# Start-up order, norm by one constant matmul, and the place of 24 modulation blocks in a two-layer diffusion backbone

## The chip, the cores and the metric

One core of a Trainium2 chip runs the whole kernel: TensorE (PE), VectorE (DVE), ScalarE (ACT), GpSimd (POOL) and the DMA queue that SyncE (SP) feeds. The metric is the device time of one execution in microseconds.

## The reference, cut to what matters

Two layers over 256 latent tokens and 256 context tokens of width 2048, all in float32. Layer 0 is a gated linear recurrence beside a short convolution, layer 1 a Hyena long convolution; a squared-ReLU mlp follows each. Every sublayer's input is normalised, scaled and shifted by a modulation vector that comes from the conditioning vector c.

```python
def rmsnorm(x, g):
    xf = x * lax.rsqrt(jnp.mean(x * x, axis=-1, keepdims=True) + EPS)
    return xf * g
for l in range(2):
    sh1, sc1, g1, sh2, sc2, g2 = split(silu(c) @ ada_w[l] + ada_b[l], 6)
    h = rmsnorm(x, norm_g[l, 0]) * (1.0 + sc1) + sh1
    if l == 0:   # the context goes through the same weights with its own modulation
        hc = rmsnorm(ctx, norm_g[0, 0]) * (1.0 + csc1) + csh1
        y = hgrn_conv_mixer(h, hc, ab_w_in, ..., ab_w_out)
    else:
        y = hyena_mixer(h, hy_in_w, ..., hy_out_w)
    x = x + g1 * y
    x = x + g2 * sq_relu_mlp(rmsnorm(x, norm_g[l, 1]) * (1.0 + sc2) + sh2, mlp_w1[l], mlp_w2[l])
return rmsnorm(x, final_g)
```

## The kernel before, in words

**Data.** Activations lie transposed: 16 k-tiles of 128 channels by 256 tokens. Every large product is three TensorE products of halves (high and low part of each operand): a weight tile of 1 MB is loaded into one of three buffers `raw`, ScalarE copies its high part (`whi`, L150) and VectorE makes the low part (`wlo`, L151). TensorE then runs high by high, high by low and low by high.

**Stages** of the profiled execution: phase 0, the first 3072 columns of ab_w_in for tokens and context (0 to 455 us); the other columns of that projection and the recurrence (to 785); its output projection (to 890); mlp(0) (to 1655); the hyena's input projection with its chain of transforms (to 2142); its output projection, called "ho" (to 2260); mlp(1) (to 3006); the last norm and the store.

**Phase 0** goes by k: `KBLOCKS` cuts the 16 k-tiles into stretches of 1, 3, 4 and 8, and each stretch adds its part to sums in SBUF (L611, L615). A stretch is a row of weight loads (L676); `block_mm` (L594, L597) multiplies each by the normalised tokens (side 0) and context (side 1). The input of k-tile kt, `h`, needs the norm of the tokens and two modulation vectors: `ada_start(kt)` loads two blocks of 1 MB and multiplies them on TensorE (L211, then L551 and L553); `h_make` turns x and the modulation into h (L562, L568, L570, L571). All k-tiles of the next stretch go through `ada_start` between the weight loads of a stretch, and `h_make` makes all of them at its end.

**Modulation blocks.** 192 blocks of 1 MB make the modulation, in the order of their index l\*96 + ch\*16 + kt. The first 32 are those of ada_start. The rest stand in a queue `ada_q` that `pump` and `pump_rate` empty at points set by hand: `RATES` says how many blocks a point takes off ("hy" in the hyena chain, "ho" in its output projection, ("m1", l) in the mlps). A block whose index is in `ON_PE` is multiplied by `ada_mm` on TensorE (L211, sums of rows L193, L194), any other by one VectorE instruction with a sum (L181). Loads (L162) go through `raw`, or in the mlps and the first output projection through two buffers of their own, `araw`. `pump_until` empties the queue up to the index that the next step needs.

**A norm** is `rstd_sum` (L324: squares times a constant column, giving 128x2), `rsqrt` (L304 to L312, integer start and three Newton steps on 128x2), and `rstd_fin` (L333: two diagonals; L337: a matmul that spreads them over all partitions). There are six: two in phase 0, and before mlp(0), the hyena, mlp(1) and the store. In phase 0 the squares of four k-tile quads are added by `qadd` (L527), one of three by GpSimd.

**The filter network** of the hyena (`filter_net`, L1053 to L1185) runs on GpSimd from the start of the kernel; `filter_tail` (L1124 on) uses it in mlp(0).

The order on each engine is the scheduler's, close to the order of the program text; loads are issued by SP in that order, and a load waits until its buffer is free.

## Time and profile before

| | us |
|---|---|
| median of three runs | 3024.0 (3020.43 to 3026.61) |
| the profiled execution, its own time | 3025.2 |
| its span in the trace | 3023.4 |
| TensorE busy | 2787.5 (92%) |
| VectorE busy | 2203.2 (73%) |
| ScalarE busy | 1241.5 (41%) |
| GpSimd busy | 1535.0 (51%) |
| mean DMA rate | 214 GB/s |

The shares are means over all stages. TensorE is nearly full over the mlps, so the stages in which it is not have to be read one by one, by windows. A row of the timeline gives the start, the duration and the engine of one or several equal instructions and, in brackets, how long the engine was idle before and what released it; an SPq row is the issue of a load and its wait for a buffer.

### The profile page before, as it was taken

The numbers are of one execution on the slowest core, as the hardware profiler recorded it, in microseconds if no ns is written. First come the engines' busy times: TensorE is split into PE (matmuls) and PEld (weight loads), VectorE is DVE, ScalarE is ACT, GpSimd is POOL, SyncE is SP. The second block draws the span as 40 slices with busy tenths as digits, with TensorE's granted clock in tenths as the row PEclk, the third lists the DMA queues.
The fourth block names the chain that finished last, engine by engine and source line by source line (L and its number), as shares of the span: only waits on it lengthen the run. The fifth ranks groups of instructions, "written<-read, shape, count | busy, mean of one in ns | idle before, by whom it ended". The sixth has DMA issues, their size and how long they took to land.

```text
span 3023.4 us, 44604 instructions
## 1 busy us (share of the span) xinstructions
PE 2787.5 (92%) x17728; PEld 2455.0 (81%) x17728; DVE 2203.2 (73%) x2632; ACT 1241.5 (41%) x1635; POOL 1535.0 (51%) x1718
## 2 busy tenths in 40 slices
PE   4887899999989999998999898889779999999997
PEld 3787899988988888887888788889777888888885
DVE  3565669998798878876778899999766555555555
ACT  3212224333445444353445454444335444344443
POOL 6999999999999999925000444554000000000000
PEclk8898899999999999999999899999999999999998
DMA  4766455445767887886876333333575555656553
GB/s 158 277 245 233 169 193 183 163 142 221 259 237 270 321 303 294 323 294 257 310 289 248 125 136 122 130 140 112 186 276 180 211 211 212 217 209 218 199 181 112
DMA packets 97569, 647.43 MB, mean 214 GB/s; under 512 B 11640, under 2 KB 15800, under 8 KB 21456
## 3 DMA queue, kind: packets, MB, share of 16 engines
q1 hardware_dynamic: 96176, 641.40, 58.2%
q0 software_dynamic: 1184, 3.18, 0.7%
q8 instruction: 139, 2.28, 0.3%
q14 instruction: 70, 0.57, 0.1%
HBM read 642.44 MB, written 2.10 MB: 213 GB/s over the span
## 4 chain that ended last, share of the span: by engine, by line
PE 64%; DVE 22%; DMA 5%; issue 3%; ACT 2%; POOL 2%; DVEq 0%; ACTq 0%; SPq 0%; POOLq 0%
PE acc L281 45%; PE acc L260 8%; DVE wlo L151 6%; PE aux L594 2%; PE acc L594 2%; DMA raw<-in_w 1%; DMA raw<-in_ho 1%; PE aux L295 1%; DVE raw L181 1%; PE aux L597 1%; DVE p L939 1%; DMA raw<-in_ada 1%; PE acc L597 1%; DVE p L937 1%; ACT whi L150 1%
## 5 line engine op out<-in xcount | busy, mean ns | idle before, releaser
L151 DVE TENSOR_TENSOR wlo<-raw,whi 128x1024 fp32r<-128x1024 f32 (+1 forms) x772 | 1011.8, 1315 | 514.2 <-ACT whi L150 509.5
L150 ACT ACTIVATE whi<-raw 128x1024 fp32r<-128x1024 f32 (+1 forms) x800 | 842.1, 1056 | 1163.3 <-PE acc L281 706.9
L1034 POOL TENSOR_TENSOR xT<-xT,rstd 128x256 f32<-128x256 f32 x6 | 5.3, 910 | 878.6 <-ACT rstd L449 878.6
L260 PE MATMUL acc<-hh,whi 128*128 128x258 f32 (+1 forms) x1408 | 406.4, 289 | 1.5 <-ACT whi L150 1.5
L260 PE MATMUL acc<-hh,wlo 128*128 128x258 f32 (+1 forms) x1408 | 400.5, 285 | 5.7 <-DVE wlo L151 5.3
L281 PE MATMUL acc<-whi,hh 128*128 128x512 f32 x1024 | 403.2, 399 | 2.2 <-ACT hh L442 2.2
L281 PE MATMUL acc<-whi,uh 128*128 128x512 f32 x1024 | 405.1, 396 | 0.0
L281 PE MATMUL acc<-whi,ul 128*128 128x512 f32 x1024 | 404.9, 395 | 0.0
L281 PE MATMUL acc<-whi,hl 128*128 128x512 f32 x1024 | 402.8, 398 | 0.2 <-DVE hl L443 0.2
L260 PE MATMUL acc<-hl,whi 128*128 128x258 f32 (+1 forms) x1408 | 398.7, 284 | 0.0
L281 PE MATMUL acc<-wlo,uh 128*128 128x512 f32 x1024 | 282.6, 396 | 8.9 <-DVE wlo L151 8.9
L281 PE MATMUL acc<-wlo,hh 128*128 128x512 f32 x1024 | 279.0, 394 | 0.0
L260 PEld LDWEIGHTS acc<-hh,wlo 128*128 128x128 f32 x1408 | 267.8, 190 | 8.5 <-DVE wlo L151 7.6
L260 PEld LDWEIGHTS acc<-hh,whi 128*128 128x128 f32 x1408 | 268.4, 191 | 6.5 <-issue 4.3
L260 PEld LDWEIGHTS acc<-hl,whi 128*128 128x128 f32 x1408 | 269.1, 191 | 0.9 <-issue 0.7
L181 DVE SCALAR_TENSOR_TENSOR araw<-araw,sil 128x2048 f32<-128x2048 f32 x102 | 249.4, 2446 | 0.0
L281 PEld LDWEIGHTS acc<-wlo,uh 128*128 128x128 f32 x1024 | 192.8, 188 | 54.7 <-DVE wlo L151 9.4
L281 PEld LDWEIGHTS acc<-whi,hh 128*128 128x128 f32 x1024 | 193.2, 189 | 47.8 <-ACT hh L442 3.7
L281 PEld LDWEIGHTS acc<-whi,hl 128*128 128x128 f32 x1024 | 193.8, 189 | 44.3 <-DVE hl L443 0.8
L281 PEld LDWEIGHTS acc<-wlo,hh 128*128 128x128 f32 x1024 | 193.0, 188 | 45.1
L281 PEld LDWEIGHTS acc<-whi,uh 128*128 128x128 f32 x1024 | 192.9, 188 | 45.0 <-issue 0.3
L281 PEld LDWEIGHTS acc<-whi,ul 128*128 128x128 f32 x1024 | 192.9, 188 | 44.5
(361 smaller groups left out, 5792.6 us busy)
## 6 DMA issues: line engine op xcount, KB each, us to landing
raw<-in_m SPq DMA_DIRECT2D x256, 1024.0 KB, 4.9
araw<-in_ada SPq DMA_DIRECT2D x102, 1024.0 KB, 5.8
raw<-in_ada SPq DMA_DIRECT2D x89, 1024.0 KB, 5.1
raw<-in_w SPq DMA_DIRECT2D x75, 1024.0 KB, 5.0
raw<-in_hy SPq DMA_DIRECT2D x48, 1024.0 KB, 4.9
raw<-in_ho SPq DMA_DIRECT2D x16, 1024.0 KB, 4.8
raw<-in_w SPq DMA_DIRECT2D x6, 768.0 KB, 6.4
raw<-in_c SPq DMA_DIRECT2D x4, 1024.0 KB, 4.7
```

Of the source, the lines that this page charges most:

```text
L150: nc.scalar.activation(out=hi[:, :w], in_=src, func=AF.Copy)
L151: e.tensor_tensor(out=lo[:, :w], in0=src, in1=hi[:, :w].bitcast(F32), op=ALU.subtract)
L181: self.hold(nc.vector.scalar_tensor_tensor(out=r, in0=r, scalar=0.5, in1=self.sil, op0=ALU.mult, op1=ALU.mult, accum_out=self.mod[:, idx:i ...
L260: m = nc.tensor.matmul(acc[:, :n], lhsT=w[:, s], rhs=x(kt, n), start=hn == 0 and j == 0 and pn == 0, stop=hn == 1 and j == 7 and pn == 2).ins
L281: nc.tensor.matmul(acc[th], lhsT=x(kt)[:, th * P:(th + 1) * P], rhs=w[:, j * 512:(j + 1) * 512], start=kt == 0 and w is hi and x is xhi, s ...
L295: nc.tensor.transpose(out=tp[:, j * T + th * P:j * T + th * P + P], in_=src[th][:, f * P:(f + 1) * P], identity=self.ident)
L594: nc.tensor.matmul(o, lhsT=w[:, e + half * P:e + half * P + P], rhs=x(kt), start=st, stop=sp)
L597: nc.tensor.matmul(o, lhsT=x(kt)[:, half * P:half * P + P], rhs=w[:, e:e + T], start=st, stop=sp)
L937: nc.vector.scalar_tensor_tensor(out=c3[:, :, 1:], in0=u3[:, :, :63], scalar=w0, in1=c3[:, :, 1:], op0=ALU.mult, op1=ALU.add)
L939: nc.vector.scalar_tensor_tensor(out=c3[:, :, :63], in0=u3[:, :, 1:], scalar=w2, in1=c3[:, :, :63], op0=ALU.mult, op1=ALU.add)
L1034: e.tensor_tensor(out=self.x[:, nt, :], in0=self.x[:, nt, :], in1=rstd, op=ALU.mult)
```

## The change

1. `KBLOCKS` becomes (1, 2, 5, 8): the second stretch has three weight loads of 1 MB, the third twelve of 0.625 MB; the fourth is as before.
2. At the beginning the first modulation blocks and weights are loaded into their own tiles (`fa`, `fw0`), and those of k-tiles 1 and 2 are issued ahead, in front of the filter network's loads. Squares and norm of the tokens come ahead of `ada_start(0)`; VectorE does all three sums; `ada_start(1)` stands ahead of the context's norm. In the stretches, `h` of a k-tile is made one weight load after its `ada_start`, for the last four on side 1 at the end of the third stretch.
3. `norm_rstd` multiplies the squares by a constant 128x128 matrix, which gives the sum on all partitions, and takes `rsqrt` at 128x256; diagonals, second matmul and copy are gone. All six norms use it.
4. Blocks 160 to 183 (of layer 1) are added to `ON_PE`. `RATES` takes 0.5 instead of 0.1 in the hyena chain and 0 instead of 1 in ho. `ada_stop` bounds what a stage may take, and `pump_to` empties up to it: 56 after phase 0, 72 before the first output projection, 160 in mlp(0), 184 in the hyena. The vector for VectorE's blocks (`make_sil`) is not made in the hyena.
5. `filter_net` is tied to the last h operation of k-tile 2 in the scheduler's order.

```diff
-KBLOCKS = (1, 3, 4, 8)
+KBLOCKS = (1, 2, 5, 8)
...
-RATES = {"gc": 0.35, "ab": 0.62, "y": 0, "gate": 0, "leash": 4, "tl": 1, "lo": 0.3, "hy": 0.1, "ho": 1.0, "ahead": 2,
+RATES = {"gc": 0.35, "ab": 0.62, "y": 0, "gate": 0, "leash": 4, "tl": 1, "lo": 0.3, "hy": 0.5, "ho": 0.0, "ahead": 2,
          ("m1", 0): 0.65, ("m2", 0): 0.65, ("m1", 1): 0.15, ("m2", 1): 0.15}
...
-ON_PE = set(range(32)) | set(range(56, 72))
+ON_PE = set(range(32)) | set(range(56, 72)) | set(range(160, 184))
...
     def pump(self, n):
         self.ada_flush()
-        while n > 0 and self.ada_q:
+        while n > 0 and self.ada_q and 192 - len(self.ada_q) < self.ada_stop:
             self.ada_block(*self.ada_q.pop(0))
             n -= 1
...
+
+    def pump_to(self, idx):
+        self.ada_stop = idx
+        self.pump(192)
+        self.ada_flush()
...
-            self.last = nc.vector.scalar_tensor_tensor(out=y, in0=q, scalar=1.5, in1=y, op0=ALU.add,
-                                                       op1=ALU.mult).ins
...
-    def rstd_row(self, sq):
-        return self.rstd_fin(self.rstd_sum(sq))
...
-    def rstd_sum(self, sq):
-        nc = self.nc
-        ms = self.psx()
-        for half in range(2):
-            for i, q in enumerate(sq):
-                nc.tensor.matmul(ms[:, half:half + 1], lhsT=q[:, half * P:(half + 1) * P], rhs=self.onesd[:, 0:1],
-                                 start=i == 0, stop=i == len(sq) - 1)
-        return ms
-
-    def rstd_fin(self, ms):
-        nc = self.nc
-        y = self.rsqrt(ms[:, :2], P, 2, "rsy")
-        dg = self.tmp(T, "sq", 2)
-        for half in range(2):
-            self.last = nc.vector.tensor_scalar(out=dg[:, half * P:(half + 1) * P], in0=self.ident,
-                                                scalar1=y[:, half:half + 1], scalar2=float(D), op0=ALU.mult,
-                                                op1=ALU.mult).ins
-        bc = self.psx()[:, :T]
-        nc.tensor.matmul(bc, lhsT=self.onesd, rhs=dg, start=True, stop=True)
-        return bc
+    def norm_rstd(self, sq):
+        ms = self.psx()[:, :T]
+        for i, q in enumerate(sq):
+            self.nc.tensor.matmul(ms, lhsT=self.onesd, rhs=q, start=i == 0, stop=i == len(sq) - 1)
+        return self.rsqrt(ms, P, T)
...
     def norm_end(self):
-        bc = self.rstd_row([self.ssum])
-        r = self.tmp(T, "rstd", 2)
-        self.nc.scalar.activation(out=r, in_=bc, func=AF.Copy)
-        return r
+        return self.norm_rstd([self.ssum])
...
+                self.pump_to(72)
+                self.ada_stop = 160
...
             self.ph = st.enter_context(tc.tile_pool(name="ph", bufs=1))
-            self.make_sil(self.ph)
+            self.ada_stop = 184
             self.hyena()
...
+            self.ada_stop = 192
...
+        fa = self.zp.tile([P, 2, D], F32, tag="z16", name="fa")
+        fw = self.zp.tile([P, 2 * D], F32, tag="z16", name="fw0")
...
             if src == "xT":
-                for ch in range(2):
-                    first.append(self.ada_load(0, ch, 0, None if ch else s8("first", [P, D])))
+                first = [self.ada_load(0, ch, 0, fa[:, ch, :]) for ch in range(2)]
...
                 for c0, cw, off in row:
-                    r = self.raw()
-                    nc.sync.dma_start(out=r[:, :cw], in_=bass.AP(w0.tensor, w0.offset + off, [[cw, P], [1, cw]]))
+                    r = fw[:, c0:c0 + cw]
+                    nc.sync.dma_start(out=r, in_=bass.AP(w0.tensor, w0.offset + off, [[cw, P], [1, cw]]))
                     loads += [(c0, r[:, g * 256:g * 256 + 1024], list(range(g, g + 4)))
                               for g in range(0, cw // 256, 4)]
+        ahead = {kt: [self.ada_load(0, ch, kt, s8("first", [P, D]) if kt == 2 and ch else None) for ch in range(2)]
+                 for kt in kb[1]}
...
-            ada_start(0, first)
             for i in range(4):
                 square(xq, qx, i)
-            qadd(nc.gpsimd, qx, 0, 1)
-            qadd(nc.vector, qx, 2, 3)
-            qadd(nc.vector, qx, 0, 2)
-            ms = self.rstd_sum([qx[0][:, j, :T] for j in range(4)])
+            for i in range(1, 4):
+                qadd(nc.vector, qx, 0, i)
+            rst.append(self.norm_rstd([qx[0][:, j, :T] for j in range(4)]))
+            ada_start(0, first)
             units = [self.wtile() for _ in loads]
             nc.scalar.activation(out=units[0][0], in_=loads[0][1], func=AF.Copy)
-            rst.append(rstd_sb(self.rstd_fin(ms)))
...
-            qadd(nc.gpsimd, qc, 0, 1)
-            qadd(nc.vector, qc, 2, 3)
-            qadd(nc.vector, qc, 0, 2)
-            ms = self.rstd_sum([qc[0][:, j, :T] for j in range(4)])
-            rst.append(rstd_sb(self.rstd_fin(ms)))
+            ada_start(1, ahead[1])
+            for i in range(1, 4):
+                qadd(nc.vector, qc, 0, i)
+            rst.append(self.norm_rstd([qc[0][:, j, :T] for j in range(4)]))
             h_make(0, 1, 1)
             for n, (c0, _, cgs) in enumerate(loads):
                 block_mm(0, 0, 1, c0, *units[n], cgs, [0], 1)
-        self.filter_net()
+            for side in range(2):
+                h_make(1, 2, side)
+            ada_start(2, ahead[2])
+            for side in range(2):
+                h_make(2, 3, side)
+        self.filter_net(self.last)
         self.sil = s8("sil", [P, D])
         sr = self.raw()
         nc.sync.dma_start(out=sr, in_=bass.AP(I["c"].tensor, I["c"].offset, [[0, P], [1, D]]))
         nc.scalar.activation(out=self.sil, in_=sr, func=AF.Tanh, scale=0.5)
         nc.vector.scalar_tensor_tensor(out=self.sil, in0=self.sil, scalar=1.0, in1=sr, op0=ALU.add, op1=ALU.mult)
-        for kt in kb[1]:
-            ada_start(kt)
-        for side in range(2):
...
         for b, (k0, nkt, row) in list(enumerate(chunks))[1:]:
             nxt = kb[b + 1][:] if b + 1 < len(chunks) else []
             nn = len(nxt)
+            made = []
             for ci, (c0, cw, off) in enumerate(row):
                 self.pump(1)
+                for kt in made:
+                    h_make(kt, kt + 1, 0)
+                    if kt < 12:
+                        h_make(kt, kt + 1, 1)
+                made = []
                 r = self.raw()
                 nel = nkt * cw
                 nc.sync.dma_start(out=r[:, :nel], in_=bass.AP(w0.tensor, w0.offset + off, [[nel, P], [1, nel]]))
                 while nxt and (nn - len(nxt)) * len(row) < nn * (ci + 1):
+                    made.append(nxt[0])
                     ada_start(nxt.pop(0))
...
-            if nn:
-                for side in range(2):
-                    h_make(kb[b + 1][0], kb[b + 1][-1] + 1, side)
-
+            for kt in made:
+                h_make(kt, kt + 1, 0)
+                if kt < 12:
+                    h_make(kt, kt + 1, 1)
+            if b == len(chunks) - 2:
+                for kt in range(12, KT):
+                    h_make(kt, kt + 1, 1)
+
+        self.pump_to(56)
+        self.ada_stop = 72
...
             for g in range(4):
+                if c == 3 and g == 2:
+                    self.pump_to(self.ada_stop)
...
         def halves(a, hi, lo):
-            gp.tensor_scalar(out=hi, in0=a, scalar1=4097.0, scalar2=None, op0=ALU.mult)
+            i = gp.tensor_scalar(out=hi, in0=a, scalar1=4097.0, scalar2=None, op0=ALU.mult)
+            if gate:
+                self.hold(i.ins, gate.pop())
...
         self.leash = None
-        self.pump_until(1, 2)
+        self.pump_to(184)
         for nt in range(KT):
```

In the instruction order this shows as follows. First TensorE at the start of the program; `first`, `raw` and `fa` are the first two modulation blocks, `sq_...` the sums of squares, `onesd` the constant matrix. Before, with the modulation products first:

```order
L211 MATMUL aux<-first,silt 32x128 x16
L211 MATMUL aux<-raw,silt 32x128 x16
L551 MATMUL aux<-selr,sq 128x2 x2
L324 MATMUL aux<-onesd,sq_175 128x1 x8
L337 MATMUL aux<-sq,onesd 128x256
L594 MATMUL aux<-hh,whi 128x256
```

The same place on TensorE after the change:

```order
L324 MATMUL aux<-sq_143,onesd 128x256 x4
L212 MATMUL aux<-fa,silt 32x128 x32
L534 MATMUL aux<-selr,sq 128x2 x2
L577 MATMUL aux<-hh,whi 128x256
L577 MATMUL aux<-hl,whi 128x256
L577 MATMUL aux<-hh,wlo 128x256
```

The norm's matmuls now stand ahead of the modulation products, and the second norm matmul (L337) is gone.

VectorE at the end of the third stretch; L568 or L551 is the x part of h, L571 or L554 its low half, L611, L615 or L598 adds a product to its sum, `x_99` to `x_118` are quads of k-tiles of the two sides. Before, with eight k-tiles made at once:

```order
L553 TENSOR_TENSOR mod<-aux,sm 128x2x2
L562 SCALAR_TENSOR_TENSOR gv<-mod,sm 128x8 x2
L568 SCALAR_TENSOR_TENSOR x_99<-x_99,gv,rstd 128x256 x4
L568 SCALAR_TENSOR_TENSOR x_101<-x_101,gv,rstd 128x256 x4
L568 SCALAR_TENSOR_TENSOR x_116<-x_116,gv,rstd 128x256 x4
L568 SCALAR_TENSOR_TENSOR x_118<-x_118,gv,rstd 128x256 x4
L571 SCALAR_TENSOR_TENSOR hl<-x_99,mod,hh 128x256
L611 TENSOR_TENSOR v<-acc,v 128x2x256
L571 SCALAR_TENSOR_TENSOR hl<-x_99,mod,hh 128x256 x3
L571 SCALAR_TENSOR_TENSOR hl<-x_101,mod,hh 128x256 x2
L611 TENSOR_TENSOR cv<-aux,cv 128x2x256
L571 SCALAR_TENSOR_TENSOR hl<-x_101,mod,hh 128x256 x2
```

On VectorE after the change, two k-tiles of the same stretch:

```order
L152 TENSOR_TENSOR wlo<-raw,whi 128x256
L545 SCALAR_TENSOR_TENSOR gv<-mod,sm 128x1 x2
L551 SCALAR_TENSOR_TENSOR x_103<-x_103,gv,rstd 128x256
L551 SCALAR_TENSOR_TENSOR x_116<-x_116,gv,rstd 128x256
L554 SCALAR_TENSOR_TENSOR hl<-x_103,mod,hh 128x256
L598 TENSOR_TENSOR zz<-acc,zz 128x256 x2
L598 TENSOR_TENSOR czz<-aux,czz 128x256 x2
L182 SCALAR_TENSOR_TENSOR raw,mod<-raw,sil 128x2048
L536 TENSOR_TENSOR mod<-aux,sm 128x2x2
L152 TENSOR_TENSOR wlo<-raw,whi 128x1024
L152 TENSOR_TENSOR wlo<-raw,whi 128x256
L545 SCALAR_TENSOR_TENSOR gv<-mod,sm 128x1 x2
```

The h operations of eight k-tiles stood in a row; now two or three stand between the sums of each weight load.

SP in the hyena's output projection; `raw<-in_ho` is a weight load, `in_ada` a modulation block, `in_m` a weight load of mlp(1), `in_c` the conditioning vector. Before:

```order
L248 DMA raw<-in_hy 128x2048 x2
L248 DMA raw<-in_ho 128x2048 x2
L162 DMA raw<-in_ada 128x2048 x2
L248 DMA raw<-in_ho 128x2048
L162 DMA raw<-in_ada 128x2048
```

The same place on SP after the change:

```order
L254 DMA raw<-in_hy 128x2048 x2
L163 DMA raw<-in_ada 128x2048
L254 DMA raw<-in_ho 128x2048 x5
L163 DMA araw<-in_ada 128x2048 x2
L254 DMA raw<-in_ho 128x2048 x11
L205 DMA raw<-in_c 128x2048
L279 DMA raw<-in_m 128x2048 x11
```

Before, ho loads and modulation blocks go on alternating like the last two rows up to the last ho load but two; now two modulation blocks stand there in all, in buffers of their own, and the loads of mlp(1) follow.

## Rows read from the trace of the kernel before

**Rows 1.** The page, part 4: the chain of waits by line.

```profile
PE acc L281 45%; PE acc L260 8%; DVE wlo L151 6%; PE aux L594 2%; PE acc L594 2%; DMA raw<-in_w 1%; DMA raw<-in_ho 1%; PE aux L295 1%; DVE raw L181 1%; PE aux L597 1%; DVE p L939 1%; DMA raw<-in_ada 1%; PE acc L597 1%; DVE p L937 1%; ACT whi L150 1%
```

**Rows 2.** Windows: length, PE, PEld, DVE, ACT, POOL busy (count), PEclk, DMA share, GB/s.

```profile
280.00:321.00 41.00, 20.50 (x161) 19.06 (x160) 29.72 (x44) 11.20 (x21) 40.03 (x61) 0.71 0.38 130
321.00:455.00 134.00, 134.00 (x1129) 134.00 (x1128) 87.61 (x105) 33.78 (x33) 130.30 (x178) 1.00 0.54 189
868.00:886.00 18.00, 17.89 (x152) 17.68 (x150) 16.44 (x18) 7.67 (x10) 17.68 (x18) 1.00 0.83 298
1690.00:2110.00 420.00, 376.32 (x2983) 367.93 (x2981) 395.27 (x531) 206.54 (x319) 206.46 (x138) 0.97 0.36 128
2142.60:2259.50 116.90, 95.15 (x693) 91.01 (x692) 75.23 (x91) 35.69 (x46) 0.00 (x0) 0.91 0.66 248
```

**Rows 3.** Timeline of the beginning: start, duration, engine, line, names.

```profile
15.16 1.93 PE L211 MATMUL aux<-first,silt 128*32 128x128 f32 x32 [15.16 <-DMA first<-in_ada]
...
19.81 3.89 ACT L524 ACTIVATE sq<-x 128x1024 f32<-128x1024 f32 x4
...
23.73 2.92 DVE L527 TENSOR_TENSOR sq<-sq,sq 128x1024 f32<-128x1024 f32 x2 [2.47 <-ACT sq L524]
...
28.13 0.40 POOL L1053 TENSOR_SCALAR fxh<-fzt 128x66 f32<-128x66 f32 x1 [3.89 <-DMA fzt<-in_zf]
...
40.11 0.58 PE L594 MATMUL aux<-hh,whi 128*128 128x256 f32 x1 [1.63 <-ACT hh L570]
```

**Rows 4.** Chain of waits from 0 to 300 us: start, duration, what.

```profile
68.42 1.96 PE acc L594 x6
...
79.13 1.93 PE aux L211 x64
```

**Rows 5.** Timeline of SP: the first weight loads of stretches two, three, four.

```profile
95.04 0.33 SPq L676 DMA_DIRECT2D raw<-in_w  x1
...
166.68 0.33 SPq L676 DMA_DIRECT2D raw<-in_w  x1
...
279.71 0.33 SPq L676 DMA_DIRECT2D raw<-in_w  x1
```

**Rows 6.** Timeline of VectorE at the end of the third stretch.

```profile
286.93 9.97 DVE L568 SCALAR_TENSOR_TENSOR x<-x,gv,rstd 128x256 f32<-128x256 f32 x16
```

**Rows 7.** Waits in the ho stage, 2142 to 2265 us: total, times, longest.

```profile
ACT whi L150 <- DMA raw<-in_ho: 62.9, 13, 6.6
```

**Rows 8.** Chain of waits where mlp(1) begins.

```profile
2255.09 7.62 DMA raw<-in_m
```

**Rows 9.** Timeline of two norms: VectorE before mlp(0), all engines at the end.

```profile
891.92 0.54 DVE L312 SCALAR_TENSOR_TENSOR rsy<-rs_q,rsy 128x2 f32<-128x2 f32 x1
...
3006.03 0.43 DVE L430 TENSOR_TENSOR ssum<-ssum,sq 128x256 f32<-128x256 f32 x1 [0.27 <-ACT sq L429]
...
3008.61 0.16 DVE L312 SCALAR_TENSOR_TENSOR rsy<-rs_q,rsy 128x2 f32<-128x2 f32 x1
...
3010.61 1.19 PE L337 MATMUL aux<-sq,onesd 128*128 128x256 f32 x2 [3.03 <-DVE sq L333]
```

**Rows 10.** Timeline of GpSimd: last filter network operation, first of the tail.

```profile
1304.06 0.47 POOL L1185 TENSOR_TENSOR fxn<-sfq,sfp 128x128 f32<-128x128 f32 x1
1370.79 0.30 POOL L1160 TENSOR_SCALAR sfp<-cv 128x128 f32<-128x128 f32 x1 [66.27 <-DVE cv L1134]
```

**Rows 11.** The DMA view, 11 to 22 us.

```profile
DMA packets 1459, 4.49 MB, mean 409 GB/s; under 512 B 97, under 2 KB 845, under 8 KB 1101
```

**Rows 12.** Groups of instructions, 1690 to 2110 us: busy, mean ns, idle before.

```profile
L181 DVE SCALAR_TENSOR_TENSOR raw<-raw,sil 128x2048 f32<-128x2048 f32 x5 | 11.4, 2284 | 0.0
```

**Rows 13.** Groups of instructions, 455 to 790 us: TensorE's modulation blocks there.

```profile
L211 PE MATMUL aux<-raw,silt 128*32 128x128 f32 x512 | 17.3, 276 | 0.0
...
L193 PE MATMUL aux<-selr,adas 128*128 128x2 f32 x30 | 4.2, 210 | 0.0
```

**Rows 14.** Chain of waits by line, 1690 to 2110 us.

```profile
by line: DVE wlo L151 11.6%; DVE p L939 6.8%; issue 6.7%; PE acc L260 6.7%; DVE yl L157 5.7%; DVE p L937 5.6%; DVE y L1333 5.2%; DVE y L1331 4.7%; DVE cv L1299 4.4%; PE aux L1210 3.5%; DVE y L1330 3.5%; DVE Z L1271 3.2%; DVE tf L1248 3.1%; 
```

More of the change, by code (lines that the diff above doesn't have):

```diff
@@ L69, in __init__ @@
         self.ada_late = []
+        self.ada_stop = 56
         self.ada_raw = None
@@ L297, in flip, with rsqrt @@
         return tp
-    def rsqrt(self, ms, rows, w, tag="rstd"):
+    def rsqrt(self, ms, rows, w):
         nc = self.nc
         v = self.tmp(w, "rs_v", 1)[:rows]
-        y = self.tmp(w, tag, 2)[:rows]
+        y = self.tmp(w, "rstd", 2)[:rows]
         q = self.tmp(w, "rs_q", 1)[:rows]
@@ L311, in rsqrt @@
             nc.vector.scalar_tensor_tensor(out=q, in0=q, scalar=-0.5, in1=v, op0=ALU.mult, op1=ALU.mult)
[L312 to L338 removed]
+            nc.vector.scalar_tensor_tensor(out=y, in0=q, scalar=1.5, in1=y, op0=ALU.add, op1=ALU.mult)
+        return y
+    def norm_rstd(self, sq):
[3 more added lines that the diff above has]
+        return self.rsqrt(ms, P, T)
     def setup(self):
@@ L433, in norm_apply @@
         nc = self.nc
-        bc = self.rstd_row([self.ssum])
+        bc = self.norm_rstd([self.ssum])
         self.new_h()
@@ L446, in norm_end @@
     def norm_end(self):
-        bc = self.rstd_row([self.ssum])
-        r = self.tmp(T, "rstd", 2)
-        self.nc.scalar.activation(out=r, in_=bc, func=AF.Copy)
-        return r
+        return self.norm_rstd([self.ssum])
     def build(self):
@@ L494, in layer0 @@
         xq, cq = [], []
-        first = []
+        fa = self.zp.tile([P, 2, D], F32, tag="z16", name="fa")
+        fw = self.zp.tile([P, 2 * D], F32, tag="z16", name="fw0")
         for lst, src in ((xq, "xT"), (cq, "ctxT")):
@@ L527, in qadd @@
             return e.tensor_tensor(out=q[i][:, :, :T], in0=q[i][:, :, :T], in1=q[j][:, :, :T], op=ALU.add).ins
-        def rstd_sb(bc):
-            r = self.tmp(T, "rstd", 2)
-            nc.scalar.activation(out=r, in_=bc, func=AF.Copy)
-            return r
         zz = self.zp.tile([P, 2, NH, T], F32, tag="z16", name="zz")
@@ L663, in layer0 @@
         nc.vector.scalar_tensor_tensor(out=self.sil, in0=self.sil, scalar=1.0, in1=sr, op0=ALU.add, op1=ALU.mult)
-        for kt in kb[1]:
-            ada_start(kt)
-        for side in range(2):
-            h_make(kb[1][0], kb[1][-1] + 1, side)
         lbt = self.lb_setup()
@@ L847, in readout @@
         def readout():
-            rr = self.rsqrt(st["msq"][:NH, :T], NH, T, "rstd")
+            rr = self.rsqrt(st["msq"][:NH, :T], NH, T)
             sel = pa.tile([NH, NH, P], F32, tag="s4", name="sel", bufs=2)
@@ L1036, in mlp_body, with filter_net @@
                     nc.sync.dma_start(out=self.out[:, nt - 3:nt + 1, :], in_=self.x[:, nt - 3:nt + 1, :])
-    def filter_net(self):
+    def filter_net(self, after):
         nc, cp, I, pm = self.nc, self.cp, self.I, self.pm
         gp = nc.gpsimd
+        gate = [after]
         zt = pm.tile([P, 2, 64], F32, tag="fx", name="fzt", bufs=2)
```

## Prediction

> **What bounds the kernel now.** I read the chain of waits by line first: half of it is TensorE working through L281 and L260, the products of the two mlps and of the projections [rows 1]. An edit that removes work of another engine beside those products is worth nothing. So I looked for stretches in which TensorE is not full, with the table by windows [rows 2]: 280 to 321 us, where it is busy 20.50 of 41; 1690 to 2110 (the hyena chain) with 376.32 of 420 while VectorE has 395.27; and 2142.6 to 2259.5 (the hyena's output projection, "ho") with 95.15 of 116.9. The last stretch of phase 0, 321 to 455, is full: 134.00 of 134. The change touches the first three of these, and the beginning up to the load at 95.04 [rows 5]. All sums are made against the profiled execution, 3025.2 us (span 3023.4); the median of the runs is 1.2 lower, and I take 1.2 off at the end. A measurement of this kernel can tell about 0.2%, 6 us, from no change.
>
> **1. The beginning up to the first weight load that has to wait.** Before, the first modulation product (15.16) stands ahead of the squares, which run on ScalarE from 19.81 for 3.89 us, 0.97 each; two VectorE sums take 2.92, 1.46 each; the first product of phase 0 starts at 40.11 [rows 3]. After, squares and norm come first. The x tiles are issued ahead of the load that ended at 15.16, so they land before it. With the last square at 14 to 15 and one sum of 1.46 behind it, the four norm matmuls can start at about 16. A 128x256 matmul at that clock cost 1.19 for the pair of passes [rows 9], so four end at about 20 at the latest. The new inverse root is twelve VectorE operations of 128x256; such an operation takes 0.43 with VectorE alone [rows 9], so 5.2. Two more (x by gain, then hh) make 1.2. First product: 26.5, between 24 (tiles early, matmuls warm) and 31 (GpSimd slowing the root). From side 0's first product to side 1's it was 68.42 - 40.11 = 28.3, and side 1's block lasts to 79.13, 10.7 [rows 3, 4]. I leave both as they are: ada_start(1) has gone in between, one more 2 us of TensorE, but the POOL sum is gone from the ctx norm. Side 1's block then ends at 65.5. The modulation loads of k-tiles 1 and 2 are issued ahead and have long landed, so their products take 1 us or so, a raw buffer falls free, and the first weight load of stretch two goes out at 66.5. Before it went out at 95.04 [rows 5], behind seven modulation loads that wait for buffers in turn.
>
> **2. Stretches two and three.** Both are paced by three raw buffers, and each load waits for one. Between the weight loads at 95.04 and 166.68 there are 20 loads, 3.58 us each; between 166.68 and 279.71 there are 28, 4.04 each [rows 5]. After, 56 loads lie between the first weight load of stretch two and the first of the last stretch (15 of weights, 41 of modulation), 51.5 MB. The pace is not shown for the new order; its ends are 4.04 and, if loads went as fast as the DMA engines can, the rate of 409 GB/s [rows 11], 2.5 us. I take 3.6, the pace of the stretch without a block of h_make at its end: what made stretch three slower is gone (next sentence). 66.5 + 56 x 3.6 = 268. Before, the weight load at 279.71 [rows 5] was followed by 9.97 us of x operations (L568) and their low halves [rows 6], with TensorE half idle to 321 [rows 2]; now the h of a k-tile is made one chunk after its modulation, and only side 1 of the last four is left for the end. So the last stretch is full about 8 us after its load, at 276.5, not at 321. Its own 134 us do not change. Gain 44.5; at 4.04 it is 20.
>
> TensorE does not stop this. A k-tile is 144 matmuls (24 column blocks, two sides, three passes), so seven are 1008, 119 us at the 0.118 of the quiet window [rows 2], and 26 modulation blocks at 17.3 / 16 = 1.08 [rows 13] are 28: 147 of 210. The GpSimd filter network starts later: 28.13 before [rows 3], when fzt landed; its load now stands behind 4 MB, about 10 us at [rows 11]. It loses two sums of its own (4.7 us), ended at 1304.5 and its follower started only at 1370.79 [rows 10]. The follower comes 44 us earlier, at 1326, against an end of about 1310: 16 us are left.
>
> **3. The norms.** Six norms change; four lie outside phase 0. Before, a quiet one is twelve 128x2 operations of 0.16 at steps of 0.2 (2.3 us in all), a matmul pair of 1.19 [rows 9], and by estimate 2 for the small matmul, the diagonals and, in two of them, a copy: 5.5. After, it is 1.2 for the matmul and twelve 128x256 operations at 0.43, 5.2: 6.4. Net +1 (hyena, end), +1.5 where there was no copy (ho to mlp). For ab_out to mlp(0) the filter network runs beside it: there the same small operation took 0.54 and not 0.16 [rows 9]. I take +2, bounds +1 and +7. The Trainium skill ("GPSIMD Engine Reference", § 1. Specifications) says that GpSimd's path to SBUF is shared with VectorE and contended by VectorE instructions with two SBUF inputs, which speaks against wide operations here; the 0.54 agrees. If each wide operation were stretched by as much as the small one there, this norm would be at +7 and the sum 5 higher. Sum without the ho one, which is counted below: 1 + 1 + 2 = +4.
>
> **4. 24 modulation blocks move.** (a) Out of "ho": ScalarE waits there 62.9 us for the ho weights, 13 times [rows 7], since 13 blocks of 1 MB stand between them in the same three buffers. Without them 693 matmuls at the full pace of the quiet window, 17.89 / 152 = 0.118 each [rows 2], are 82 us, against 116.9: a gain of 35 at most. I take 31, and 25 if the landings are not covered at the start. Behind it, the mlp weights were waited for 7.62 us in the chain [rows 8]; they are now issued behind ho loads alone. I count half of that, -3, and the norm's +1.5: -1.5. (b) Into the hyena: five VectorE blocks of 2.28 [rows 12] go, 11.4, and 24 blocks on TensorE come. One costs 1.08 and 4.2 / 15 = 0.28 for its row sums [rows 13], 1.36; 24 are 33 us. VectorE carries about three quarters of the chain there and TensorE about a fifth (its largest lines are VectorE's) [rows 14], and TensorE has 44 us of waits for VectorE to put them in [rows 2]: +7 - 6 = +1. Bounds: -8 if all hides, +33 if none does. (c) mlp(1) loses eight VectorE blocks and mlp(0) gains two: nothing, since L281 hides them there [rows 1]; were that cover gone, 2.3 each.
>
> **Sum.** -44.5 + 4 - 31 - 1.5 + 1 = -72: 2953.2 for the profiled execution, 2952 against the median.
>
> **The rivals.** A, the pace stays 4.04 although the h_make block is gone, because the three buffers are held by VectorE's modulation blocks in turn: stretch two and three take 226, phase 0 gains 20, and the time is 2976. For: 28 loads ran so. Against: that stretch contains the h_make gap. B, the 24 blocks lie on the path in the hyena: its TensorE would have 376.32 + 33 = 409 of 420, so there is hardly room for waits of its own; +32, 2984. Against: the waits of TensorE are for VectorE, and an ada product needs nothing of it. C, loads go at the DMA rate as soon as squares and h no longer hold buffers; then phase 0 is bound by products, and the GpSimd filter network caps the gain at 61 (1370.79 - 1310): 2936. The row shows 409 GB/s for loads without a buffer to wait for. The Trainium skill ("DMA: Bandwidth & Descriptors", Specifications) gives about 358 GB/s as a core's HBM limit; the trace is above it, and by 358 the loads would take 144 us, which is still less than TensorE's 147, so it would not change C.
>
> D, slower: every modulation block in the hyena stands in TensorE's queue ahead of the next projection product, and its 1 MB is issued only when one of three raw buffers is free, so TensorE waits a landing for each. A landing that the chain shows there is about 4.8 (the ho waits, 62.9 / 13) [rows 7]: 24 x 4.8 = 115, 3067. It turns to slower above 73 / 24 = 3.0 us a block. Against: the blocks are issued a step ahead, and DMA in that stretch is busy 0.36 [rows 2].
>
> E, the change does not do what it says in one place: the filter network's first operation, which the text ties to the last h operation, also waits for it. In the order, GpSimd waits there for its load alone. If it did wait, it would start some 44 us later than before, end near 1344, and the follower, due at 1326, would be 18 late: 2970.
>
> **How the numbers follow.** Forecast 0.60, 2952, its own range 2935 to 2970 (pace 3.3 to 3.8, ho 25 to 35, hyena -8 to +15). A 0.16, B 0.10, C 0.05, D 0.05, E 0.04. The range 2928 to 2987 takes in all but D, the far side of C and A with B together. Faster by over 0.2%: all but D and a small part of A with B, 0.93; within 0.2%: 0.02; slower: 0.05.
>
> **What would show it.** First product at 24 to 31; weight load of stretch two near 66 and of the last stretch near 268; TensorE full from about 276 and no block of L551 in its front; the ho stage near 86 us with few waits of ScalarE for in_ho; the hyena stretch within -8 and +15 of 420, with TensorE's waits for VectorE shrunk by what the blocks take; norms 5 to 6 us of root. It is wrong if loads in stretch three are 4 us apart or more, if TensorE waits in the hyena for in_ada, or if the filter's follower waits for GpSimd.

## The result, and the profile after

The changed kernel takes 2976.46 us (median of 4, 2974.1 to 2978.21), before 3025.27: a ratio of 0.9841, 95% interval 0.9824 to 0.9858, so 48.8 us faster. The forecast was 2952, 72 to 73 faster. The profiled execution took 2974.1 with a span of 2972.0, against 3025.2 and 3023.4 before, so the two traces differ by 51.4.

The page of the changed kernel, its part 1: TensorE is busy as long as before (2787.5 us) in a shorter span.

```profile
PE 2790.1 (94%) x18508; PEld 2457.8 (83%) x18508; DVE 2176.5 (73%) x2648; ACT 1246.6 (42%) x1660; POOL 1565.0 (53%) x1716
```

Where the 51.4 went is read from six marks in the traces, each the start of a TensorE line or of the last output of the hyena chain (us). The gain against before stands in brackets. "e1" and "e2" are the first two experiments below: the block move alone, and everything else alone.

| mark | before | after | e1, move alone | e2, the rest alone |
|---|---|---|---|---|
| first product of the projection's second part (phase 0 is over) | 451.2 | 429.4 (21.8) | 448.6 (2.6) | 431.9 (19.3) |
| first product of mlp(0) | 897.8 | 875.6 (22.2) | 895.6 (2.2) | 879.1 (18.7) |
| first product of the hyena's projection | 1643.2 | 1629.1 (14.1) | 1639.3 (3.9) | 1635.9 (7.3) |
| last output of the hyena chain (zo) | 2143.4 | 2124.9 (18.5) | 2132.7 (10.7) | 2136.8 (6.6) |
| first product of mlp(1) | 2270.3 | 2217.4 (52.9) | 2223.8 (46.5) | 2268.6 (1.7) |
| span | 3023.4 | 2972.0 (51.4) | 2976.5 (46.9) | 3024.2 (-0.8) |

So phase 0 gained half of what was forecast, mlp(0) took 8 of it away, the hyena chain gained 4, and ho with the norm behind it gained 34. The gain of the part without the move is nearly gone by the end (e2; the execution profiled there was the slowest of ten, 3025.99 against a median of 3020.41, so its last marks show some 5 us too little).

**The beginning and phase 0.** The timeline of TensorE and of SP: the first product, and the first weight loads of stretch two and of the last stretch; they answer to [rows 3] and [rows 5].

```profile
25.56 0.58 PE L577 MATMUL aux<-hh,whi 128*128 128x256 f32 x1 [2.86 <-ACT hh L553]
```

```profile
72.12 0.33 SPq L663 DMA_DIRECT2D raw<-in_w  x1
```

```profile
281.80 0.33 SPq L663 DMA_DIRECT2D raw<-in_w  x1
```

The first product came 1 us before the forecast (26.5). The weight load came at 72.1 and not at 66.5. The 56 loads between these two took 209.7 us, 3.74 each. The windows of the last stretch, of the hyena chain and of ho (columns as in [rows 2]) follow:

```profile
285.00:295.00 10.00, 8.83 (x67) 8.63 (x67) 10.00 (x16) 3.04 (x4) 9.76 (x13) 0.91 0.54 201
295.00:429.00 134.00, 134.00 (x1129) 134.00 (x1128) 77.18 (x99) 33.87 (x32) 130.16 (x190) 1.00 0.49 169
1674.00:2092.00 418.00, 393.53 (x3682) 380.44 (x3681) 385.24 (x546) 211.14 (x343) 202.47 (x137) 0.99 0.47 173
2124.90:2211.00 86.10, 82.83 (x689) 81.84 (x687) 52.40 (x66) 39.12 (x49) 0.00 (x0) 1.00 0.61 219
```

TensorE is full from 295, not from 276.5 as forecast and not from 321 as before [rows 2]. From there to the mark of the table it is 134 us, and was 130 before, when some products of the last stretch were done ahead of 321.

**ho.** It is 86 us with TensorE busy 82.8, as forecast. In the groups of instructions of 2124.9 to 2212 us the wait of ScalarE for the ho loads [rows 7] is gone; it now waits for the products:

```profile
L151 ACT ACTIVATE whi<-raw 128x1024 fp32r<-128x1024 f32 x30 | 31.6, 1059 | 44.7 <-PE acc L266 42.7 <-issue 2.0
```

**The hyena chain.** The modulation products there (groups of instructions, 1674 to 2092 us, with 22 of the 24 blocks) wait for no load at all, and TensorE's waits from 1640 to 2125 us have none for a modulation block either:

```profile
L212 PE MATMUL aux<-raw,silt 128*32 128x128 f32 x704 | 25.5, 283 | 1.8 <-DVE p L1346 1.7
```

**mlp(0).** Its waits of TensorE from 1300 to 1400 us have a new row, and GpSimd's timeline shows the other side of it (to be laid beside [rows 10]; `fxn` is the last output of the filter network, which the tail takes up):

```profile
PE aux L1127 <- POOL fxn L1184: 4.7, 1, 4.7
```

```profile
1348.23 0.45 POOL L1184 TENSOR_TENSOR fxn<-sfq,sfp 128x128 f32<-128x128 f32 x1
1358.45 0.30 POOL L1159 TENSOR_SCALAR sfp<-cv 128x128 f32<-128x128 f32 x1 [9.77 <-DVE cv L1133]
```

Before, GpSimd had been done with fxn for 66 us when its follower could start. Now TensorE stands still for it, and the 66 us have become 9.77, the time from fxn through TensorE and VectorE to the follower.

### The profile page after: what moved, and what is told of

It is laid out like the page before. It is cut to its first block, busy times and chain, and to the rows that moved or that the text cites. A ratio compares the mean times of both kernels' runs of the same rounds, so it can differ in the third digit from the quotient of the medians.

```text
span 2972.0 us, 46189 instructions
## 1 busy us (share of the span) xinstructions
PE 2790.1 (94%) x18508; PEld 2457.8 (83%) x18508; DVE 2176.5 (73%) x2648; ACT 1246.6 (42%) x1660; POOL 1565.0 (53%) x1716
## 5 line engine op out<-in xcount | busy, mean ns | idle before, releaser
L182 DVE SCALAR_TENSOR_TENSOR araw<-araw,sil 128x2048 f32<-128x2048 f32 x96 | 237.9, 2479 | 0.2 <-DMA araw<-in_ada 0.2
```

The source lines that it names most:

```text
L182: self.hold(nc.vector.scalar_tensor_tensor(out=r, in0=r, scalar=0.5, in1=self.sil, op0=ALU.mult, op1=ALU.mult, accum_out=self.mod[:, idx:i ...
```

## Experiments

**e1: the move of the 24 blocks alone.** Theory: the parts add up, and the trace's stages tell what each is worth. Rival: one of them needs another.

```diff
 # kernel before
-ON_PE = set(range(32)) | set(range(56, 72))
+ON_PE = set(range(32)) | set(range(56, 72)) | set(range(160, 184))
-"hy": 0.1, "ho": 1.0
+"hy": 0.5, "ho": 0.0
+# ada_stop, pump_to and the stops as in the change
```

> The kernel before with the move of the 24 modulation blocks alone (ON_PE, RATES, the stops of the queue); beginning, stretches and norms as before. Theory 1, the parts add up and this one carries most of the gain: from the stages of the two traces, ho -33.4, the boundary behind it -2.5, the hyena chain -6.6: about -42, 2983 us. Theory 2, the hyena's -6.6 came with the new norm or the earlier front, and the blocks there cost as much as they free: -34, 2991. Theory 3, the ho stage gains only because of the front: above 3005.

Measured: 2974.36 us, ratio 0.9835 (0.9818 to 0.9851). This is the time of the whole change, 2976.46. By the table the hyena chain, from its first product to zo, takes 493.4 instead of 500.2, so 6.8 less, and from zo to mlp(1) it is 91.1 instead of 126.9, 35.8 less. Theory 1 holds, with a little more than it expected. TensorE's busy time in the hyena window shows why the 33 us of products cost nothing:

```profile
1690.00:2110.00 420.00, 398.67 (x3730) 385.92 (x3729) 390.66 (x556) 215.09 (x347) 209.78 (x141) 1.00 0.47 174
```

It rose from 376.3 [rows 2] by 22 with a granted clock of 1.00 instead of 0.97. Over the whole stage, from the first product to zo, it rose by 23 (438.5 to 461.6), though the 24 blocks took 34 (27.1, and 7.0 for their row sums); TensorE's waits for VectorE fell from 43 to 19, and the other products took 11 us less, at a granted clock of 0.98 and not 0.95. So the blocks went into waits for VectorE, and the clock rose with it; no run parts the two.

**e2: everything but that move.**

```diff
 # changed kernel
-ON_PE = ... | set(range(160, 184))
-"hy": 0.5, "ho": 0.0
+"hy": 0.1, "ho": 1.0
-            self.ada_stop = 184
+            self.ada_stop = 192
+            self.make_sil(self.ph)
-        self.pump_to(184)
+        self.pump_until(1, 2)
```

> The changed kernel with the 24 modulation blocks put back where they were (VectorE, 0.1 in the hyena, 1 in ho); beginning, stretches and norms as changed. Theory 1, the front's -21.8 at the end of phase 0 shrinks by the norms and by the wait for the filter network to about -9 at the end: 3016 us. Theory 2, the front keeps its gain: 3003 us. The first product of the second part of the projection should start at about 429 us in either, as in the changed kernel.

Measured: 3020.41 us, ratio 0.9984 (0.9974 to 0.9994), 4 us of gain. Phase 0 ends 19 us earlier, and at the first product of mlp(1) 1.7 are left. Theory 1 holds, with 4 us of gain where it had 9: 11 go in mlp(0), and 5 between zo and mlp(1), in ho with its thirteen blocks and the longer norm behind it.

**e3: one SBUF input instead of two.** In the changed kernel the x operation of the norms ahead of the mlps reads rstd from SBUF; before it read PSUM. This kernel puts the result back into PSUM.

```diff
 # changed kernel, rsqrt, only for norm_apply
+            o = ms if back and n == 2 else y
-            nc.vector.scalar_tensor_tensor(out=y, in0=q, scalar=1.5, in1=y, ...)
+            nc.vector.scalar_tensor_tensor(out=o, in0=q, scalar=1.5, in1=y, ...)
```

> The changed kernel; the last Newton operation of the two norms ahead of the mlps writes its result into PSUM, and the x operations behind it (L427) read it there, so that they have one input in SBUF and not two. Theory 1, the x operations beside the busy GpSimd fall back from 743 ns to 470, and the 4 us that mlp(0) loses at its start come back: 2972 us. Theory 2, they fall back, but TensorE only arrives earlier at the filter tail and waits there for GpSimd: 2976, no change. Theory 3, the second input is not the reason: durations stay at 743 ns.

The groups of instructions at the start of mlp(0), before, changed and e3 (x count, busy us, mean ns):

```profile
L440 DVE SCALAR_TENSOR_TENSOR cv<-xT,gv,aux 128x256 f32<-128x256 f32 x16 | 6.9, 471 | 1.4 <-PE aux L337 1.4
```

```profile
L427 DVE SCALAR_TENSOR_TENSOR cv<-xT,gv,rstd 128x256 f32<-128x256 f32 x16 | 11.3, 743 | 0.0
```

```profile
L428 DVE SCALAR_TENSOR_TENSOR cv<-xT,gv,aux 128x256 f32<-128x256 f32 x16 | 6.9, 469 | 0.0
```

The second SBUF input costs 272 ns an operation while GpSimd is busy; in mlp(1), where GpSimd is idle, the two kernels have 479 and 475. Theory 1's mechanism is shown, for the operations; what it is worth in time is not. The Trainium skill ("GPSIMD Engine Reference", § 1. Specifications) says that such instructions contend with GpSimd, and the trace agrees. The time was 2973.18 (0.9827, 0.9811 to 0.9843), 3 less than the changed kernel, which the intervals do not separate; TensorE still waits 3.2 us for fxn, as theory 2 had it in part.

**e4: the filter network starts 10 us earlier.**

```diff
 # changed kernel: zf, fb1, fb2, freq, fw3, f3v loaded first
+        self.filter_loads()
         ahead = {kt: [self.ada_load(0, ch, kt, ...) for ch in range(2)] for kt in kb[1]}
```

> The changed kernel with the loads of the filter network issued ahead of the modulation loads of k-tiles 1 and 2. GpSimd should start at about 28 us and not at 38. Theory 1, the filter network ends on the path of mlp(0) and its late start costs the 4.7 us that TensorE waits for fxn: 2972 us, and no such wait. Theory 2, VectorE's work beside GpSimd sets the network's end and not its start: 2976, the wait remains.

Measured: 2970.09 us, ratio 0.9826 (0.9803 to 0.9848), 6 less than the changed kernel. GpSimd starts at 28.22 and not at 38.33, TensorE has no wait for fxn any more, and from mlp(0)'s first product to the hyena's it is 746.8 instead of 753.5. Theory 1 holds by the trace; by the time it is not clear, since the intervals overlap.

```profile
28.22 0.74 POOL L1092 TENSOR_TENSOR fp<-fzt,fw 128x256 f32<-128x256 f32 x1 [18.55 <-DMA fzt<-in_zf]
```

**e5: the stretches of before.**

```diff
 # changed kernel
-KBLOCKS = (1, 2, 5, 8)
+KBLOCKS = (1, 3, 4, 8)
-         for kt in kb[1]}
+         for kt in (1, 2)}
+        ada_start(3)
+        for side in range(2):
+            h_make(3, 4, side)
```

> The changed kernel with the stretches of before, (1, 3, 4, 8) k-tiles; the new start, the h operations one weight load after their modulation, norms and blocks as changed. Read in the trace by the first product of the second part of the projection (451 us before, 429 changed). Theory 1, the new cut of the stretches is what makes the first weight load go out early and carries some 10 us: 439. Theory 2, it is the early start and the spread of the h operations, and the cut carries nothing: 429. The time at the end should move by less than 5 us either way, since what phase 0 gains is given back in mlp(0).

Both theories fall. Phase 0 ends at 406.2, 23 us *earlier* than with the new cut. The timeline of SP, first weight loads of stretch two and of the last stretch:

```profile
80.76 0.33 SPq L666 DMA_DIRECT2D raw<-in_w  x1
```

```profile
260.22 0.33 SPq L666 DMA_DIRECT2D raw<-in_w  x1
```

These are 48 loads in 179.5 us, 3.74 each, the pace of the changed kernel. The new cut has eight more loads at that place (three more weight loads, two more modulation blocks of ada_start, three more blocks of VectorE), 30 us, and lets the first load go out 8.6 earlier. It is a loss. Still, the time at the end is 2980.71, because TensorE (1300 to 1450 us) waits:

```profile
PE aux L1130 <- POOL fxn L1187: 32.0, 1, 32.0
```

27 more than in the changed kernel, for the 23 gained. That wait also shows that the network's pace follows the work beside it. These are the windows of the network's last 88 instructions, up to the end of fxn, here and in the changed kernel (columns as in [rows 2]):

```profile
1290.40:1353.40 63.00, 30.99 (x139) 24.96 (x137) 27.36 (x23) 16.57 (x21) 59.91 (x88) 0.78 0.47 176
1251.00:1348.70 97.70, 93.04 (x415) 75.44 (x413) 75.84 (x63) 45.43 (x55) 94.62 (x88) 1.00 0.79 303
```

The same 88 instructions took 63 us while the other engines stood still for a good part of it (VectorE busy 27 us), and 98 us while they did not (VectorE busy 76). ScalarE and the DMA engines do less in the first window too, so that it is VectorE that slows GpSimd is not isolated.

**e6: no VectorE modulation blocks in stretches two and three.**

```diff
 # changed kernel
-                self.pump(1)
+                self.pump(2 if b == len(chunks) - 1 else 0)
```

> The changed kernel with no VectorE modulation blocks in stretches two and three of phase 0; all 24 go into the last stretch, two for each weight load. 15 of the 56 loads between 72 and 282 us are gone. Theory 1, the three buffers pace these stretches at 3.74 us a load: 41 loads take 153, the last stretch begins 56 us earlier, and the first product of the second part of the projection, 429 in the changed kernel, starts at about 375. Theory 2, TensorE at its granted clock and its waits for h pace them (it is busy 172 of 210): at most 30 us earlier, 400 or later. Theory 3, the 36 loads of the last stretch pace that in turn: no earlier than 425. The time at the end: 2976 in all three if GpSimd's filter network ends on the path, since TensorE then waits for it longer.

The first weight load of stretch two now goes out at 41.26, and the next load 30 us behind it, at 71.57. The last stretch's first weight load (timeline of SP) goes out 49 us earlier than in the changed kernel:

```profile
232.44 0.33 SPq L663 DMA_DIRECT2D raw<-in_w  x1
```

From 71.57 on these are 42 loads in 160.9 us, 3.83 each. The windows of stretches two and three, and of the last one:

```profile
82.00:250.00 168.00, 164.03 (x1900) 157.66 (x1893) 109.91 (x201) 43.45 (x72) 163.94 (x267) 0.97 0.68 247
241.00:417.00 176.00, 147.89 (x1139) 145.86 (x1138) 111.13 (x127) 32.13 (x32) 171.51 (x221) 0.89 0.55 207
```

In the first, TensorE is nearly full, so at 3.8 us a load the products are as long as the loads; the 49 us lie between theory 1 (56) and theory 2 (at most 30). In the second it is not full any more, since the blocks went there: from that load to the end of phase 0 it is 185 us and not 148 (theory 3 in part). Phase 0 ends at 417.5, 12 earlier. The time is 2976.88: TensorE's wait for fxn is 12.6 longer than in the changed kernel.

```profile
PE aux L1127 <- POOL fxn L1184: 17.3, 1, 17.3
```

**e9: old norm outside phase 0, early filter loads.** If the front was eaten by the network's end and by the norms, then without the two it must come out.

```diff
 # e4
-        bc = self.norm_rstd([self.ssum])
+        bc = self.rstd_row([self.ssum])     # sums, 128x2 root, diagonals, second matmul, as before
 # the same in norm_end, with the copy to SBUF
```

> The changed kernel with the old norm at the four places outside phase 0 and the filter network's loads ahead of the modulation loads of k-tiles 1 and 2. Theory 1, the front's gain of some 20 us was given back by the filter network's late end (4.7), by the x operations with two SBUF inputs (4) and by the longer norms (some 4 together): 2963 us, 11 below the move of the blocks alone. Theory 2, the gain goes away somewhere else: 2970 or more.

Measured: 2952.26 us, ratio 0.9757 (0.9734 to 0.9781), 24 below the changed kernel and 22 below e1. That is the whole of phase 0's gain. The norms were worth more than expected, about 18 between the medians of e4 and e9. By the marks of the kernels with the 24 blocks moved, six with either norm: 4 at the start of mlp(0) (e3), some 5 in the hyena (495.5 to 498.2 us from its first product to zo with the new norm, 489.6 to 493.4 with the old), some 2 ahead of mlp(1) (91.9 to 93.0 from zo against 90.2 to 91.6), 1 at the end. Together that is about the 12.6 between the traces of e4 and e9 (spans 2963.2 and 2950.6), whose first products of mlp(0) stand at 870.3 and 870.4. The other 5 of the 18 have no place in the kernel: e4's profiled execution was the fastest of its four (2965.12 to 2976.07).

**e13: the filter tail later, nothing else.**

```diff
 # changed kernel, mlp_body
-                if c == 2 and g == 0 and l == 0:     # ahead of the second product
-                    self.filter_tail()
+                if c == 3 and g == 0 and l == 0:     # ahead of the first product
+                    self.filter_tail()
```

> The changed kernel with the filter tail 16 groups of products later in mlp(0) (at the start of its last quarter and not in the second half of its third). Theory 1, TensorE's 4.7 us wait for GpSimd's fxn is all that the filter network costs: 2972 us, no such wait. Theory 2, the tail's own work then ends too late for the hyena, and that begins with a wait: 2976 or more.

Measured: 2965.09 us, ratio 0.9808 (0.9791 to 0.9824), 11 less than the changed kernel, and still a wait:

```profile
PE aux L1127 <- POOL fxn L1184: 3.6, 1, 3.6
```

Neither theory fits. In the traces 10.9 of the 11 us are there at the first product of mlp(0) already (864.7 against 875.6), ahead of anything that this edit touches; the later tail only let them through. TensorE came to it 492 us behind that product and not 468, 107 of its instructions further on, while fxn ended at 1360 and not at 1348. At 468 it would have come at 1333, by estimate from these numbers 15 us before fxn ended in the changed kernel. And phase 0 ended at 419.9 in this execution, with the instruction order of phase 0 that the changed kernel has (429.4); in e2 and e3, with the same order, it ended at 431.9 and 435.6. The end of phase 0 thus scatters by some 8 us to either side between kernels with one order, and marks of phase 0 that differ by less say nothing. Whole executions of one kernel can lie closer (the four of e9 within 3 us), so what scatters is open.

**e10, e11, e12, e14: both fixes, then the stretches of before, the tail later, fewer loads, the tail later again.**

```diff
 # e10 = e9 with KBLOCKS = (1, 3, 4, 8) as in e5
 # e11 = e10 with the tail as in e13
 # e12 = e11 and, in phase 0:
-                self.pump(1)
+                self.pump((0, 1, 0, 1 + ci % 2)[b])
 # e14 = e12 and, in mlp_body:
-                if c == 3 and g == 0 and l == 0:
+                if c == 3 and g == 2 and l == 0:
```

> The kernel with the old norm outside phase 0 and the early filter loads (2952 us), and with the stretches of before, (1, 3, 4, 8). 48 loads and not 56 lie between the first weight loads of stretch two and of the last stretch. Theory 1, phase 0 ends 20 us earlier (406 and not 427), and TensorE waits the same 20 us more for the filter network, which ends at 1333 as before: 2952 us. Theory 2, that network ends earlier with phase 0: 2932.

> The same with the filter tail later in mlp(0), so that the network's end has some 80 us to spare. Theory 1, the 20 us that the cut of the stretches gives in phase 0 now reach the end: 2932 us. Theory 2, they are lost in another place: 2945 or more.

> The same, and the VectorE modulation blocks of stretch three (6) go to the last stretch, which takes one and two in turn. 42 loads and not 48 lie between the first weight loads of stretch two and of the last stretch. Theory 1, the pace of 3.7 us a load holds: the first product of the second part of the projection starts up to 20 us earlier than 406, at 386, and the time is some 12 to 20 us less, 2915 us. Theory 2, TensorE is nearly full in these stretches by then (171 of 192 us): 10 us at most, 2922. Theory 3, the 30 loads of the last stretch pace that: no gain, 2932.

> The last kernel (stretches of before, no VectorE blocks in stretch three, old norm outside phase 0, early filter loads) with the filter tail yet half a quarter of mlp(0) later; in the order its first product stands some 360 TensorE instructions further on, about 50 us. There TensorE waited 11.2 us for fxn, although phase 0 ended at 401 and not at 414. Theory 1, that wait was the last thing that the filter network cost: it is gone, and the time falls by about 11 us to 2933. Theory 2, the tail then ends too late for the hyena, which waits for it: 2944 or more.

| kernel | phase 0 ends | wait for fxn | us | ratio (95%) |
|---|---|---|---|---|
| e9 | 426.9 | none | 2952.26 | 0.9757 (0.9734 to 0.9781) |
| e10 | 410.7 | 9.7 | 2957.07 | 0.9776 (0.9757 to 0.9796) |
| e11 | 414.4 | none | 2942.68 | 0.9727 (0.9713 to 0.9742) |
| e12 | 401.5 | 11.2 | 2944.58 | 0.9736 (0.9722 to 0.9751) |
| e14 | 400.2 | none | 2929.37 | 0.9682 (0.9666 to 0.9698) |

The waits of TensorE, 1300 to 1450 us, in e10 and in e12:

```profile
PE aux L1155 <- POOL fxn L1212: 9.7, 1, 9.7
```

```profile
PE aux L1155 <- POOL fxn L1212: 11.2, 1, 11.2
```

Each time phase 0 ends earlier without room behind it, TensorE waits for fxn and nothing is gained (e10 against e9, e12 against e11); with room the gain arrives (e11, e14). e11 gave 10 against e9 where 20 were expected, since its phase 0 ended at 414 and not at 406, within the scatter. In e11 TensorE came to the tail 8 us after fxn was done, not some 80 as expected, so that e12, 13 us earlier, ran into it. None of e12's theories had the network come back as the limit; that is what e14 tested, with TensorE at the tail 112 us further behind mlp(0)'s first product, and its theory 1 held: 15 us less than e12, where it had 11. e14 beats the changed kernel by 47 us.

## Why the prediction was right, and where not

**The move of the blocks** was right in mechanism, and it was worth more than forecast. Without the norm's +1.5 the forecast is -31 in ho, -3 behind it and +1 in the hyena, together -33. e1 shows -50 by the medians and -46.9 by the trace: -35.8 from zo to mlp(1), -6.8 in the hyena (bounds -8 and +33). There nearly all of the blocks hid. The step "VectorE three quarters, TensorE a fifth" charged TensorE's share for work that went into its waits, and took off 6 where three quarters of 11.4 are 8.6. Rivals B and D fall with it: no modulation product waited for its load. This move alone is worth 50 us, which is what the whole change is worth.

**Phase 0, -44.5 forecast, -21.8 measured** (-15.6 to -31.3 in the four kernels with this order). The first product (26.5, measured 25.6) was right. The first weight load was 5.6 late. The pace was taken as 3.6 and was 3.74, 8 us over 56 loads (3.59 to 3.77 in the four kernels). From the last stretch's first load to a full TensorE it was 13 and not 8.5. Together they are the 18.5 between 295 and 276.5. (By a full TensorE the gain is 26, by the mark of the table 21.8: before, some products of the last stretch were done ahead of 321.) The larger fault is one of reading: the sum showed that the new cut has 56 loads where there had been 48, and the prediction did not ask what those eight cost. With the old cut phase 0 ends 23 us earlier in e5, and 16 and 12 earlier in e10 and e11 against e9: that much of the phase's gain is lost by the cut.

**The filter network, "16 us are left".** This step failed, and it decides the result. In e5 phase 0 ends 45 us earlier than before, which is the forecast gain of 44.5, and the time is 2980.71 all the same. The start moved by 10 us as forecast (28.13 to 38.33), but the network, 1276 us long before, was 1310 long, with as many GpSimd instructions and VectorE busy 1047 us during its life and not 995. That its pace follows the work beside it is shown by the windows under e5; that VectorE's added work makes up the 34 us was not tested by a run of its own. That its end bounds mlp(0) is shown: e5, e6, e10 and e12 by the wait, e4 and e14 by its absence. The prediction had set this down as a sign of being wrong (the follower waits for GpSimd). Rival C had named this cap, at 61 us of gain in phase 0; it lies near 17 (21.8 less the wait of 4.7). Rival E had the mechanism too, with another reason for it; GpSimd did start when its load landed.

**The norms, +4 and +1.5 forecast.** Place by place they cost about 12 (4 at mlp(0), 5, 2, 1), as between the traces of e4 and e9. The norm itself was cheap at mlp(0): from the last sum of squares to the first product it took 9.4 us and not 8.8, 0.6 where +2 was forecast. The step missed that the wide rstd lies in SBUF, so that also the sixteen x operations behind it get a second SBUF input (e3). Why the hyena loses 5 is not shown.

**The rivals.** 2976 was the time of rival A, and phase 0 gained about what A gave it (20), but not for A's reason: the pace was 3.74, not 4.04, and the pace's 8 us alone would have left 2960. Between the traces 20.6 of the forecast 72 are missing: phase 0 fell short by 22.7 and mlp(0) lost 8.1, while the hyena, ho and the stage between phase 0 and mlp(0) came out 10.7 better than forecast. So it is luck that the errors nearly cancel and the time, outside the forecast's own range of 2935 to 2970, still lies within 2928 to 2987. One sum in rival C is off: a block of 128x2048 in float32 has 1,048,576 bytes, so its 51.5 MB are 54.0 million bytes, and at 358 GB/s they take 151 us and not 144, more than TensorE's 147 and not less. Nothing measured turns on it.

## What to carry to other kernels

A front that ends earlier is worth only what the next engine that runs through the whole of it can follow: before counting a gain, write down the slack of every long chain on a slow engine, and let its length grow with the work that is pushed beside it. Where loads go through a few shared buffers, count loads: here each cost 3.6 to 3.95 us whatever its order, so that a cut into other stretches is judged by how many loads it leaves in the paced part. That the number of buffers sets this pace was not tested: no run changed it. And work can be moved to the engine that waits, even to one that is 90% busy, if its waits are for the engine that is relieved.

## What was not expected of the hardware

Between the first weight loads of stretch two and of the last stretch, loads through three buffers of 1 MB took 3.85 us each before (48 loads), 3.74 in the changed kernel (56) and in e5 (48), and 3.59 (e13, 56) to 3.95 (e11, 48) in the others; in e6 it is 3.83 from its second load on (42). A VectorE operation of 128x256 with a second SBUF input took 743 ns beside a busy GpSimd, 469 with that input in PSUM, and 479 with two SBUF inputs and GpSimd idle. The same 88 GpSimd instructions took 63 us beside engines that mostly stood still and 98 us beside busy ones. And the end of phase 0 scattered between 420 and 436 us in four kernels with the same instruction order there.
